# Token sums kept whole in DRAM and loaded ahead, two gate pairs held on chip, and a reset order in a decoder block on one core

## The chip, the core and the metric

The kernel runs on one core of one Trainium2 chip. The core has four compute engines that run their own instruction streams in order: TensorE (PE, matrix products; the page lists its weight loads apart as PEld), VectorE (DVE), ScalarE (ACT) and GpSimd (POOL). SyncE (SP) issues most of the transfers between DRAM and on-chip memory, POOL and ACT can issue some too. The metric is the device time of one execution in microseconds, lower is better, as the median of several runs. Time before: 1531.62 us (three runs, 1530.86 to 1532.0).

## What is computed

One decoder block over 1024 tokens with 16 learned meta tokens ahead (1040 positions of width 1024), all in float32:

```python
h = layer_norm(concat([meta, x]), ln0)
u_s5, q, k, v, o_pre, i_pre, f_pre, g_s5, g_m = split(h @ w_in + b_in)
z    = gelu(s5(u_s5)) @ s5_w_glu                  # grouped complex state-space scan
y_s5 = z[..., :D] * sigmoid(z[..., D:])
q, k = silu(causal_conv(q, k))                    # 4 taps
hm   = head_norm(mlstm(q, k, v, i_pre, f_pre))    # chunkwise, 4 heads
y_m  = (sigmoid(o_pre) * hm) @ m_w_out
mix  = sigmoid(g_s5) * y_s5 + sigmoid(g_m) * y_m
h    = layer_norm(ALPHA * h + mix @ w_o, ln1)
h    = layer_norm(ALPHA * h + square(relu(h @ w_up + b_up)) @ w_down, ln2)
return h without the meta positions
```

## The kernel before, in words

**Precision.** Each large product is made of float32 parts that PE takes: a number x is split into a high part (an ACT copy to the rounded type) and a low part (a DVE subtract, x minus its high part). A product is then three matmuls, high by high (L254), low by high (L255) and high by low (L256). Weights arrive raw (`wraw`), and ACT and DVE split them (`split_act`, L984 and L985: `gmwh` high, `gmwl` low; L234 and L235: `whi`, `wlo`). The activations after the first layer norm are kept on chip, transposed, as `hT_hi` and `hT_lo`, and also whole in DRAM as `h_dr`.

**Jobs.** The combined projection is cut into jobs that run one after the other in the order of the table `ORDER`: `q0` to `q3` (query and key), `v0` to `v3`, `u0` to `u3` (input of S5), `o0` to `o7` (some output gates), and the twelve pairs of gate tiles of which `a4` to `a11` and `b4` to `b11` treat eight. The GLU products (`glu`), the output products of the mLSTM (`ym`) and the two feed-forward matrices follow.

**Gate pairs by seven products.** A pair p of weight tiles against four quarters of the tokens is computed with seven products instead of eight, from sums of weight quarters (`wsums`) and sums of token quarters. Job `a{p}` loads the raw weights, forms the weight sums, writes two of them (`n1`, `r1`) to `gw_dr`, and runs products 1 to 3: 1 leaves an intermediate in `gme` (ACT), 2 gives a finished quarter that goes through a sigmoid into the buffer `gso` (one buffer) and from there to `sig_dr`, 3 adds to the intermediate (DVE), which goes to `e_dr`. Job `b{p}` loads `gw_dr` (two transfers of 512 KB) and `e_dr` back, splits the weights, and runs products 6, 5, 4 and 7, whose sums DVE adds into `gme` and `gmx`; ACT applies the sigmoid and SP writes to `sig_dr`. Product 4 of a job runs inside the next b-job.

**Token sums.** The generator `t_prep` makes the four token sums from `h_dr` early in the kernel (four chunks: load `tpr`, `quarter_sums` on DVE, split on ACT and DVE into `tpo`, write 512 KB to `t_dr`). Where the a-jobs end, `hT_hi` and `hT_lo` are overwritten block by block with these sums: `t_load(n)` loads the high and the low part of sum n from `t_dr`, 1 MB each, issued on POOL, straight into their place. Products 1, 2 and 3 of the last three a-jobs (`TAIL`) are therefore run block by block across the three jobs (all products 2, then all products 3), with a `t_load` behind each block.

**Work beside the jobs.** Other work is put between the matmuls by "lanes" of generators: the convolution (`cv`, first tap by ACT, three by DVE), the mLSTM (`ml`; `hraw` is its output, normalised in halves on ACT and DVE), S5 (`s5`, `s5c`; `s5Mx<-s5Kt` are 16 small transfers on SP, `s5Z`, `s5T`, `s5w` its scans on DVE), `t_prep` and `ah_scale` (`ah`), the gating of the mLSTM output (`hg`) and early work on the up matrix (`up`). `PACE`, the lists `ML` to `Y5` and `TPW` say how much matmul time passes between two steps of a lane, `LANE_AT` at which job a lane starts. On each engine the instructions then run in program order, but for a priority offset that a few places set; tiles come from a shared pool of slots of 30 buffers, and an instruction that takes a slot waits for its last user.

**Head.** The tables `LOAD0` (order of the first loads: x tiles, constants, weights) and `LN0_PROG` (the instructions of the first layer norm, written out by hand: s statistics, g aggregate, q root, c Newton step, n normalise, T transposes, a or v evacuation by ACT or DVE, X warm-up transposes of the identity, M matmuls of the first jobs) set the first 40 us.

Of the kernel before, what the change touches and what calls it, by code (L numbers as in the profile page):

```python
# [52 lines left out]
ML = [2.875, 1.882, 2.242, 5.227]  # L53
NL = [0.405, 2.68, 1.573, 2.414]
C5 = [1.273, 1.307, 2.211, 0.57]
K5 = [0.432, 8.726, 1.267, 8.96]
Z5 = [1.092, 0.624, 1.003, 0.401]
D5 = [3.696, 1.28, 0.806, 0.265]
W5 = [3.019, 1.105, 5.553, 0.851]
Y5 = [2.738, 1.285, 2.648, 4.789]  # L60
# [18 lines left out]
BLK = ((0, 256), (256, 640), (640, 1040))  # L79
BLK0 = (  # L80
# [49 lines left out]
def decoder_block(  # L130
# [24 lines left out]
    def f32(ap):  # L155
        return ap.bitcast(F32)
# [112 lines left out]
    t_dr = dram.tile([4, P, 2, 4, 512], F32, name="t_dr")  # L269
# [789 lines left out]
    def t_prep():  # L1059
        for c in range(4):  # L1060
            r = [slot("tpr"), slot("tpr")]
            for i in range(2):
                c0 = META + (c + 4 * i) * P
                nc.sync.dma_start(r[i][:, :D].rearrange("p (k s) -> p k s", k=KT), h_dr[:, :, c0:c0 + P])
            yield TPW
            quarter_sums(r[0], r[1])
            yield 3.0
            for n, x in ((2, r[1][:, 512:1024]), (3, r[1][:, 0:512]), (1, r[0][:, 0:512]), (4, r[0][:, 512:1024])):
                o = slot("tpo", F32R)
                a_.activation(o[:, 0:512], x, AF.Copy)  # L1070
                v_.tensor_tensor(o[:, 512:1024], x, f32(o[:, 0:512]), op=OP.subtract)
# [30 lines left out]
    def gate_out(p, i, half, x):  # L1102
        nc.sync.dma_start(sig_dr[2 * p + i, :, 512 * half:512 * half + 512], x)

    GA, GB = {}, {}

    def ga_prep(p):
        def prep(raw):
            r0, r1 = raw
            n1, n2 = wsums(r0[:, 0:512], r0[:, 512:1024], r1[:, 0:512], r1[:, 512:1024])  # L1110
            nc.sync.dma_start(gw_dr[p, 0], n1[:, :D])
            nc.sync.dma_start(gw_dr[p, 1], r1[:, :D])
            hi, lo = split_act(r0, "gmw")
            o = slot("gmo", F32R)
            a_.activation(o[:, 0:512], n2[:, 0:512], AF.Copy)
            v_.tensor_tensor(o[:, 512:1024], n2[:, 0:512], f32(o[:, 0:512]), op=OP.subtract)
            return {1: (hi[:, 0:512], lo[:, 0:512]), 2: (hi[:, 512:1024], lo[:, 512:1024]), 3: halves(o)}
        return prep

    def ga_step(p, n):  # L1120
        w, e, ps = GA[p]
        if n == 1:
            GA[p][2] = ps = mmps()
            gate_mm(ps, w[1], 0, 0, True)
            a_.activation(e[:, 0:512], ps, AF.Copy)
        elif n == 2:
            gate_mm(ps, w[2], 1, 0, False)
            x = mid.tile([P, 512], F32, tag="gso", bufs=1, name="gso")
            a_.activation(x, ps, AF.Sigmoid, bias=bft[:, gate_tile(p):gate_tile(p) + 1])
            gate_out(p, 0, 0, x)  # L1130
        else:
            px = mmps()
            gate_mm(px, w[3], 1, 1, True)
            v_.tensor_tensor(e[:, 512:1024], px, e[:, 0:512], op=OP.add)
            nc.sync.dma_start(e_dr[p], e[:, :D])

    def ga_job(p):
        def run(job):
            GA[p] = [job.w, slot("gme"), None]
            if p == TAIL[0]:  # L1140
                t_load(2)
            if not A_AFT:
                job.after()
# [99 lines left out]
    def ln0_load(t):  # L1243
        c0, n = rows0(t)
        xt = slot("x0")
        if t == 0:
            nc.sync.dma_start(xt[:META, :D], meta)
            nc.sync.dma_start(xt[META:, :D], x[0:P - META, :])
# [843 lines left out]
```

## Time and profile before

| | |
|---|---|
| median of three runs | 1531.62 us |
| the profiled execution | 1530.02 us |
| its span | 1528.3 us |
| mean granted clock of TensorE | 0.995 |
| busy: PE, DVE, ACT, POOL | 98%, 70%, 42%, 7% of the span |
| transferred | 324.92 MB, 213 GB/s mean |

The busy share tells how much of the span an engine was executing. An engine at 98% can be sped up only where it idles, so one looks for the stretches with idle time, then for what ended each wait. The granted clock is the share of full speed that the throttle allowed. A row of a timeline gives start, duration, engine, line, operation, output and inputs, and in brackets the idle time before it with the engine or transfer that ended it. The prediction quotes those rows.

### The profile page before, as it was taken

The numbers are of one execution on the slowest core, as the hardware profiler recorded it, in microseconds if no ns is written. First come the engines' busy times: TensorE is split into PE (matmuls) and PEld (weight loads), VectorE is DVE, ScalarE is ACT, GpSimd is POOL, SyncE is SP. The second block draws the span as 40 slices with busy tenths as digits, with TensorE's granted clock in tenths as the row PEclk, the third lists the DMA queues.
The fourth block names the chain that finished last, engine by engine and source line by source line (L and its number), as shares of the span: only waits on it lengthen the run. The fifth ranks groups of instructions, "written<-read, shape, count | busy, mean of one in ns | idle before, by whom it ended". The sixth has DMA issues, their size and how long they took to land.

```text
span 1528.3 us, 20822 instructions
## 1 busy us (share of the span) xinstructions
PE 1503.1 (98%) x7604; PEld 1270.7 (83%) x7604; DVE 1064.4 (70%) x1966; ACT 647.8 (42%) x1024; POOL 104.8 (7%) x178
## 2 busy tenths in 40 slices
PE   9999999999999799999999999999999999999997
PEld 9999989998888578888888888888888888888886
DVE  7487855786978665476677675766666689756786
ACT  6634552425345344332253253444444524433340
POOL 0000011523204100000000001000000000000000
PEclk9999999999999999999999999999999999999999
DMA  9417560405749998999692247544443897766642
GB/s 326 139 47 206 170 208 32 143 6 180 241 155 343 310 369 320 372 338 360 238 391 84 96 128 251 193 152 145 151 144 131 285 380 269 257 228 228 213 170 107
DMA packets 164343, 324.92 MB, mean 213 GB/s; under 512 B 19896, under 2 KB 70528, under 8 KB 164240
## 3 DMA queue, kind: packets, MB, share of 16 engines
q1 hardware_dynamic: 156992, 304.18, 58.0%
q0 software_dynamic: 7248, 19.40, 4.2%
q8 instruction: 60, 0.98, 0.3%
q14 instruction: 43, 0.35, 0.1%
HBM read 210.54 MB, written 111.81 MB: 211 GB/s over the span
## 4 chain that ended last, share of the span: by engine, by line
PE 89%; DMA 5%; DVE 2%; ACT 1%; SPq 1%; POOL 1%; issue 1%; DVEq 0%; POOLq 0%; ACTq 0%
PE mm L256 21%; PE mm L254 21%; PE mm L255 21%; PE sd L254 6%; PE sd L255 6%; PE sd L256 6%; PE mm L250 2%; DMA x<-in_x_dram 1%; PE pn L524 1%; PE pn L525 1%; PE pu L528 1%; DMA hm_dr<-hmF 1%; DMA tpr<-h_dr 1%; DMA s5yc<-ys_dr 1%; DMA ys_dr<-s5Y 1%
## 5 line engine op out<-in xcount | busy, mean ns | idle before, releaser
L254 PE MATMUL mm<-hT_hi,whi 128*128 128x512 f32 (+3 forms) x416 | 153.9, 370 | 0.0
L256 PE MATMUL mm<-hT_hi,wlo 128*128 128x512 f32 (+3 forms) x416 | 151.9, 366 | 0.0
L255 PE MATMUL mm<-hT_lo,whi 128*128 128x512 f32 (+3 forms) x416 | 151.5, 364 | 0.0
L255 PE MATMUL sd<-dwl,dah 128*128 128x512 f32 (+1 forms) x256 | 98.9, 386 | 0.0
L254 PE MATMUL sd<-dwh,dah 128*128 128x512 f32 (+1 forms) x256 | 98.9, 387 | 0.0
L256 PE MATMUL sd<-dwh,dal 128*128 128x512 f32 (+1 forms) x256 | 98.5, 385 | 0.0
L1785 ACT ACTIVATE dah<-da 128x1024 fp32r<-128x1024 f32 x56 | 58.6, 1051 | 90.2 <-PE sd L255 39.9
L1789 ACT ACTIVATE dwh<-wdr 128x1024 fp32r<-128x1024 f32 x56 | 58.9, 1053 | 79.3 <-DMA wdr<-in_wdn_dram 29.9
L255 PEld LDWEIGHTS mm<-hT_lo,whi 128*128 128x128 f32 x416 | 78.3, 188 | 10.6 <-issue 0.7
L254 PEld LDWEIGHTS mm<-hT_hi,whi 128*128 128x128 f32 x416 | 78.3, 188 | 9.9
L256 PEld LDWEIGHTS mm<-hT_hi,wlo 128*128 128x128 f32 x416 | 78.1, 188 | 10.0
L1786 DVE TENSOR_TENSOR dal<-da,dah 128x1024 fp32r<-128x1024 f32 x56 | 68.1, 1219 | 23.5 <-ACT dah L1785 23.5
L254 PE MATMUL mm<-hT_hi,gmwh 128*128 128x512 f32 x192 | 77.7, 407 | 5.0 <-ACT gmwh L984 2.5
L256 PE MATMUL mm<-hT_hi,gmwl 128*128 128x512 f32 x192 | 76.6, 404 | 5.3 <-DVE gmwl L985 5.3
L255 PE MATMUL mm<-dwl,dah 128*128 128x512 f32 (+1 forms) x208 | 80.0, 385 | 0.0
L254 PE MATMUL mm<-dwh,dah 128*128 128x512 f32 (+1 forms) x208 | 79.9, 385 | 0.0
L256 PE MATMUL mm<-dwh,dal 128*128 128x512 f32 (+1 forms) x208 | 79.7, 384 | 0.0
L255 PE MATMUL mm<-hT_lo,gmwh 128*128 128x512 f32 x192 | 76.6, 399 | 0.0
L1790 DVE TENSOR_TENSOR dwl<-wdr,dwh 128x1024 fp32r<-128x1024 f32 x56 | 68.2, 1219 | 10.2 <-ACT dwh L1789 9.6
L256 PE MATMUL mm<-whi,hT_lo 128*128 128x256 f32 (+1 forms) x256 | 74.4, 291 | 0.0
L254 PE MATMUL mm<-whi,hT_hi 128*128 128x256 f32 (+1 forms) x256 | 73.9, 289 | 0.0
L255 PE MATMUL mm<-wlo,hT_hi 128*128 128x256 f32 (+1 forms) x256 | 73.8, 288 | 0.0
(494 smaller groups left out, 3960.9 us busy)
## 6 DMA issues: line engine op xcount, KB each, us to landing
da<-act_dr SPq DMA_DIRECT2D x56, 512.0 KB, 5.2
wdr<-in_wdn_dram SPq DMA_DIRECT2D x56, 512.0 KB, 5.4
wraw<-in_wf_dram SPq DMA_DIRECT2D x36, 512.0 KB, 6.2
wur<-in_wup_dram SPq DMA_DIRECT2D x32, 512.0 KB, 4.4
act_dr<-upy SPq DMA_DIRECT2D x64, 256.0 KB, 2.7
wu_dr<-wpre SPq DMA_DIRECT2D x21, 512.0 KB, 5.4
wpre<-wu_dr POOLq DMA_DIRECT2D x21, 512.0 KB, 5.6
t_dr<-tpo SPq DMA_DIRECT2D x16, 512.0 KB, 5.2
```

The source lines that it names most:

```text
L250: t_.matmul(ps, tm[i], tm[j], start=(w == 0 and k == 0), stop=(w == 2 and k == n - 1))
L254: t_.matmul(ps, ah, bh, start=(i == 0 and part[0]), stop=False, skip_group_check=skip)
L255: t_.matmul(ps, ah, bl, start=False, stop=False, skip_group_check=skip)
L256: t_.matmul(ps, al, bh, start=False, stop=(i == n - 1 and part[1]), skip_group_check=skip)
L524: t_.matmul(pn[:, :257], qi[:, c0:c0 + n], Cs[c][:, :257], start=True, stop=False)
L525: t_.matmul(pn[:, :257], sws[c], vt[c][:, :257], start=False, stop=True)
L528: t_.matmul(pu[:, :257], kws[c][:n], vt[c][:n, :257], start=True, stop=True)
L1785: a_.activation(ah[:, :D], a[:, :D], AF.Copy)
L1786: v_.tensor_tensor(alo[:, :D], a[:, :D], f32(ah[:, :D]), op=OP.subtract)
L1789: a_.activation(wh, raw[i], AF.Copy)
L1790: v_.tensor_tensor(wl, raw[i], f32(wh), op=OP.subtract)
```

## The change

- The token sums are written to `t_dr` whole (256 KB instead of 512 KB a write); the split moves from `t_prep` to `t_load`. `t_fetch` loads a sum on SP into two slots `ttr`, one block ahead, and `t_load` splits them (two ACT copies and two DVE subtracts of 128x1024 per sum, with a priority offset) into the block of `hT_hi` and `hT_lo` that was just used.
- `HELD`: the pairs of the first two b-jobs, where they belong to `TAIL`, keep `n1`, `r1` and `gme` in their slots; nothing of them is written to or read from `gw_dr` and `e_dr`.
- `ORDER`: o1 before o0; the a-jobs end with a7 a8 a11 a10 a9 (were a8 a7 a9 a10 a11); the b-jobs run b10 b11 b9 b5 b8 b6 b4 b7 (were b4 b9 b5 b10 b8 b6 b7 b11). `t_prep` starts at q3 instead of v1, and several paces and start points are other numbers.
- The first convolution tap and all `hraw` normalisations go to DVE.
- Head: x0 comes in two column halves, with the meta rows issued on ACT; the other loads are in another order; the warm-up transposes are 41 + 18 + 1 instead of 57 + 20; some evacuations move from ACT to DVE.

```diff
-ORDER = '... o0 o1 ... u3 a8 a7 a9 a10 a11 b4 b9 b5 b10 b8 b6 b7 b11'
-HMO_AT = 2
+ORDER = '... o1 o0 ... u3 a7 a8 a11 a10 a9 b10 b11 b9 b5 b8 b6 b4 b7'
+HMO_AT = 1
+HOLD = 2
+TF = 1
+TFA = 1
+TLA = 0
+T_UP = 200
-UPD = 1
-TPW = 4.0
+UPD = 0
+TPW = 6.0
-LANE_AT = {'t_prep': 'v1', 'hm_gate': 'b5', 'ah_scale': 'glu2', 'up_early': 'ym3'}
-PACE = {'ml': 0.56, 'cv': 0.315, 's5': 1.0, 's5c': 0.729, 's5g': 2.2, 'ah': 1.549, 'up': 0.623, 'hg': 2.974}
+LANE_AT = {'t_prep': 'q3', 'hm_gate': 'b9', 'ah_scale': 'glu2', 'up_early': 'ym2'}
+PACE = {'ml': 0.56, 'cv': 0.08, 's5': 1.0, 's5c': 0.656, 's5g': 2.2, 'ah': 1.961, 'up': 0.685, 'hg': 2.974}
...
-CV0 = 1
-HRA = 1
+CV0 = 0
+HRA = 0
-LOAD0 = "x0 c0 w0 x1 w1 c1 x2 w2 x3 w3 x4 x5 x6"
+LOAD0 = "x0 c0 x1 w1 x2 w0 c1 w2 x3 w3 x6 x5 x4"
...
@@ t_prep
-                o = slot("tpo", F32R)
-                a_.activation(o[:, 0:512], x, AF.Copy)
-                v_.tensor_tensor(o[:, 512:1024], x, f32(o[:, 0:512]), op=OP.subtract)
-                nc.sync.dma_start(t_dr[n - 1, :, :, :, c * P:(c + 1) * P],
-                                  f32(o[:, 0:1024]).rearrange("p (h k s) -> p h k s", h=2, k=4))
-                yield 1.2
+                nc.sync.dma_start(t_dr[n - 1, :, :, c * P:(c + 1) * P], x.rearrange("p (k s) -> p k s", k=4))
+            yield 1.2
...
+    TR = {}
+
+    def t_fetch(n):
+        TR[n] = [slot("ttr"), slot("ttr")]
+        for j, r in enumerate(TR[n]):
+            nc.sync.dma_start(r[:, :D].rearrange("p (k s) -> p k s", k=2), t_dr[n - 1, :, 2 * j:2 * j + 2, :])
+
     def t_load(n):
         kh, half = TB[n]
         c = slice(META + 512 * half, META + 512 * half + 512)
-        for z, x in enumerate((hT_hi, hT_lo)):
-            g_.dma_start(x[:, 4 * kh:4 * kh + 4, c], t_dr[n - 1, :, z])
+        with tc.high_priority(offset=T_UP):
+            for j, r in enumerate(TR.pop(n)):
+                d = slice(4 * kh + 2 * j, 4 * kh + 2 * j + 2)
+                r3 = r[:, :D].rearrange("p (k s) -> p k s", k=2)
+                a_.activation(hT_hi[:, d, c], r3, AF.Copy)
+                v_.tensor_tensor(hT_lo[:, d, c], r3, f32(hT_hi[:, d, c]), op=OP.subtract)
+        later = [2, 1, 3, 4][[2, 1, 3, 4].index(n) + TF:]
+        if later:
+            t_fetch(later[0])
...
@@ ga_prep
-            nc.sync.dma_start(gw_dr[p, 0], n1[:, :D])
-            nc.sync.dma_start(gw_dr[p, 1], r1[:, :D])
+            if p in HELD:
+                HELD[p] = [n1, r1]
+            else:
+                nc.sync.dma_start(gw_dr[p, 0], n1[:, :D])
+                nc.sync.dma_start(gw_dr[p, 1], r1[:, :D])
...
@@ ga_job
-            if p == TAIL[0]:
+            if p == T_AT[0]:
+                for n in [2, 1, 3, 4][:TF]:
+                    t_fetch(n)
+            if p == T_AT[1]:
                 t_load(2)
...
@@ ln0_load
-            nc.sync.dma_start(xt[:META, :D], meta)
-            nc.sync.dma_start(xt[META:, :D], x[0:P - META, :])
+            for c0, c1 in HALF:
+                a_.dma_start(xt[:META, c0:c1], meta[:, c0:c1])
+                nc.sync.dma_start(xt[META:, c0:c1], x[0:P - META, c0:c1])
...
+    A_ALL = [int(w[1:]) for w in ORDER.split() if w[0] == "a"]
+    TAIL = A_ALL[-3:]
+    T_AT = A_ALL[-3 - TFA], A_ALL[-3 - TLA]
+    HELD.update({p: None for p in [int(w[1:]) for w in ORDER.split() if w[0] == "b"][:HOLD] if p in TAIL})
```

The order in which the instructions now stand shows in three places. The first is PE's order in the head, from the second row of the program on; `warm` are the warm-up transposes, `ln` the transposes of x tiles 0 (`x_109`), 1 (`x_115`) and so on. Before:

```order
L1331 MATMUL warm<-ident 128x128 x57
L1305 MATMUL ln_219<-ident,x_109 128x128 x4
L1305 MATMUL ln_220<-ident,x_109 128x128 x4
L1331 MATMUL warm<-ident 128x128 x20
L1305 MATMUL ln_270<-ident,x_115 128x128 x4
L1305 MATMUL ln_271<-ident,x_115 128x128 x4
```

Now, at the same place:

```order
L1360 MATMUL warm<-ident 128x128 x41
L1334 MATMUL ln_205<-ident,x_109 128x128 x4
L1334 MATMUL ln_206<-ident,x_109 128x128 x4
L1360 MATMUL warm<-ident 128x128 x18
L1334 MATMUL ln_250<-ident,x_115 128x128 x4
L1360 MATMUL warm<-ident 128x128
L1334 MATMUL ln_251<-ident,x_115 128x128 x4
```

The two large warm-up blocks are shorter, and one warm-up transpose stands between the halves of tile 1.

The second is SP's queue where the a-jobs end: `sig_dr<-gso` is the write of a finished gate quarter, `s5Mx<-s5Kt` the small S5 transfers. Before:

```order
L831 DMA s5Mx<-s5Kt 16x4x64 x2
L831 DMA s5Mx<-s5Kt 16x4x48 x2
L831 DMA s5Mx<-s5Kt 16x4x32 x2
L831 DMA s5Mx<-s5Kt 16x4x16 x2
L1103 DMA sig_dr<-gso 128x512
L216 DMA wraw<-gw_dr 128x1024 x2
L1165 DMA gme<-e_dr 128x1024
```

Now, up to the first of the s5Mx transfers and a little beyond:

```order
L1118 DMA sig_dr<-gso 128x512
L1156 DMA e_dr<-gme 128x1024
L221 DMA wraw<-in_wf_dram 128x1024 x2
L1091 DMA ttr<-t_dr 128x1024 x2
L1118 DMA sig_dr<-gso 128x512
L836 DMA s5Mx<-s5Kt 16x4x128 x2
L836 DMA s5Mx<-s5Kt 16x4x112
L1129 DMA gw_dr<-wus 128x1024
L1130 DMA gw_dr<-wraw 128x1024
```

The write of that gate quarter stands ahead of the s5Mx transfers, the loads of the weights and intermediate of the first b-job are gone, and loads of token sums (`ttr`) stand ahead of it.

The third is DVE's order in the first b-jobs: `gme` and `gmx` are sums of products, `gmwl` low parts of weights, `s5w` and `s5Z` S5's sums and scans. Before, in the job b4 (`gme_5590`):

```order
L1184 TENSOR_TENSOR gme_5590<-mm_5828,gme_5590 128x512
L888 TENSOR_TENSOR s5Z_5679<-s5w_5741,s5w_5742 128x520
L889 TENSOR_TENSOR s5Z_5679<-s5w_5741,s5w_5742 128x520
L894 SCALAR_TENSOR_TENSOR s5w_5741<-s5_r8_2992,s5Z_5679 128x130 x4
L1187 TENSOR_TENSOR gme_5590<-mm_5847,gme_5590 128x512
L894 SCALAR_TENSOR_TENSOR s5w_5741<-s5_r8_2992,s5Z_5679 128x130 x4
L904 TENSOR_TENSOR s5Z_5679<-s5w_5741,s5T_5617 128x512
L907 TENSOR_TENSOR s5w_5742<-s5w_5741,s5T_5617 128x512
L985 TENSOR_TENSOR gmwl_5821<-wraw_5585,gmwh_5820 128x1024
```

Now, in the job b10 (`gme_5480`), with the last subtract of token sum 4 (`hT_lo`) ahead:

```order
L888 TENSOR_TENSOR s5w_5687<-s5Z_5619,s5T_5551 128x520
L891 TENSOR_TENSOR s5w_5688<-s5Z_5619,s5T_5551 128x520
L1101 TENSOR_TENSOR hT_lo_89<-ttr_5664,hT_hi_88 128x2x512
L889 TENSOR_TENSOR s5w_5688<-s5Z_5619,s5T_5551 128x520
L890 TENSOR_TENSOR s5w_5687<-s5Z_5619,s5T_5551 128x520
L1212 TENSOR_TENSOR gme_5480<-mm_5772,gme_5480 128x512
L893 TENSOR_TENSOR s5Z_5619<-s5w_5687,s5w_5688 128x520
L894 TENSOR_TENSOR s5Z_5619<-s5w_5687,s5w_5688 128x520
L1215 TENSOR_TENSOR gme_5480<-mm_5791,gme_5480 128x512
L899 SCALAR_TENSOR_TENSOR s5w_5687<-s5_r8_2930,s5Z_5619 128x130 x5
L990 TENSOR_TENSOR gmwl_5765<-wus_5316,gmwh_5764 128x1024
L899 SCALAR_TENSOR_TENSOR s5w_5687<-s5_r8_2930,s5Z_5619 128x130 x3
```

The S5 block still stands among the sums of the first b-job; a token-sum subtract is new ahead of them, and the low weight part that follows is that of the second b-job, taken from a held tile (`wus_5316`).

More of the change, by code (lines that the diff above doesn't have):

```diff
@@ L40 @@
 MAGIC = 1.5 * 2 ** 23
-ORDER = 'q0 q1 v0 v1 q3 q2 o0 o1 o3 v2 o2 u0 u1 v3 o5 u2 o4 o7 a5 a6 a4 o6 u3 a8 a7 a9 a10 a11 b4 b9 b5 b10 b8 b6 b7 b11'
-HMO_AT = 2
+ORDER = 'q0 q1 v0 v1 q3 q2 o1 o0 o3 v2 o2 u0 u1 v3 o5 u2 o4 o7 a5 a6 a4 o6 u3 a7 a8 a11 a10 a9 b10 b11 b9 b5 b8 b6 b4 b7'
+HMO_AT = 1
 HS = 2
+HOLD = 2
[3 more added lines that the diff above has]
+T_UP = 200
 HGD = 2
-UPD = 1
-TPW = 4.0
+UPD = 0
+TPW = 6.0
 S5_START = 'o2'
-LANE_AT = {'t_prep': 'v1', 'hm_gate': 'b5', 'ah_scale': 'glu2', 'up_early': 'ym3'}
-PACE = {'ml': 0.56, 'cv': 0.315, 's5': 1.0, 's5c': 0.729, 's5g': 2.2, 'ah': 1.549, 'up': 0.623, 'hg': 2.974}
+LANE_AT = {'t_prep': 'q3', 'hm_gate': 'b9', 'ah_scale': 'glu2', 'up_early': 'ym2'}
+PACE = {'ml': 0.56, 'cv': 0.08, 's5': 1.0, 's5c': 0.656, 's5g': 2.2, 'ah': 1.961, 'up': 0.685, 'hg': 2.974}
 SPLIT_UP = 50
@@ L52 @@
 ZD = 1
[L53 to L60, printed above, removed]
-CV0 = 1
-HRA = 1
+ML = [2.875, 1.694, 2.242, 5.227]
+NL = [0.324, 2.948, 1.416, 2.414]
+C5 = [1.146, 1.176, 1.99, 0.23]
+K5 = [0.475, 9.599, 1.742, 10.842]
+Z5 = [1.081, 0.618, 0.993, 0.496]
+D5 = [3.696, 1.28, 0.645, 0.254]
+W5 = [3.019, 1.105, 4.998, 0.681]
+Y5 = [2.738, 0.771, 2.648, 4.789]
+CV0 = 0
+HRA = 0
 A_AFT = 0
@@ L268, in decoder_block @@
     h_dr = dram.tile([P, KT, LEN], F32, name="h_dr")
-    t_dr = dram.tile([4, P, 2, 4, 512], F32, name="t_dr")
+    t_dr = dram.tile([4, P, 4, 512], F32, name="t_dr")
     e_dr = dram.tile([12, P, 1024], F32, name="e_dr")
@@ L1103, in gate_out @@
         nc.sync.dma_start(sig_dr[2 * p + i, :, 512 * half:512 * half + 512], x)
-    GA, GB = {}, {}
+    GA, GB, HELD = {}, {}, {}
     def ga_prep(p):
@@ L1134, in ga_step @@
             v_.tensor_tensor(e[:, 512:1024], px, e[:, 0:512], op=OP.add)
-            nc.sync.dma_start(e_dr[p], e[:, :D])
+            if p in HELD:
+                HELD[p].append(e)
+            else:
+                nc.sync.dma_start(e_dr[p], e[:, :D])
     def ga_job(p):
@@ L1162, in gb_prep @@
     def gb_prep(p, raw):
-        n1, r1 = raw
-        e = slot("gme")
-        nc.sync.dma_start(e[:, :D], e_dr[p])
+        if p in HELD:
+            n1, r1 = HELD[p][:2]
+            e = None
+        else:
+            n1, r1 = raw
+            e = slot("gme")
+            nc.sync.dma_start(e[:, :D], e_dr[p])
         (h1, l1), (h2, l2) = split_act(n1, "gmw"), split_act(r1, "gmw")
@@ L1204, in run @@
             last = list(GB)
-            GB[p] = dict(w=job.w, e=job.w.pop("e"))
+            GB[p] = dict(w=job.w, e=job.w.pop("e") or HELD[p][2])
             if not B_AFT:
@@ L1216, in run @@
                 gb_flush()
-        all_jobs.append(Job([(gw_dr[p, i], 1024) for i in range(2)], run))
+        all_jobs.append(Job([] if p in HELD else [(gw_dr[p, i], 1024) for i in range(2)], run))
         all_jobs[-1].prep = lambda raw: gb_prep(p, raw)
@@ L1420, in up_early @@
                 yield 3.0
-    TAIL = [int(w[1:]) for w in ORDER.split() if w[0] == "a"][-3:]
+    A_ALL = [int(w[1:]) for w in ORDER.split() if w[0] == "a"]
+    TAIL = A_ALL[-3:]
+    T_AT = A_ALL[-3 - TFA], A_ALL[-3 - TLA]
+    HELD.update({p: None for p in [int(w[1:]) for w in ORDER.split() if w[0] == "b"][:HOLD] if p in TAIL})
     B_END = [int(w[1:]) for w in ORDER.split() if w[0] == "b"][-1]
```

20 rows, old and new, of the table LN0_PROG are left out of this document.

## The prediction

> **What bounds the kernel now.** The page's first two parts, read first, show TensorE (PE) as the bound.
>
> ```profile
> PE 1503.1 (98%) x7604; PEld 1270.7 (83%) x7604; DVE 1064.4 (70%) x1966; ACT 647.8 (42%) x1024; POOL 104.8 (7%) x178
> PE   9999999999999799999999999999999999999997
> ```
>
> Only one inner slice is a 7, so I asked for busy time by stretch around it (PE, PEld, DVE, ACT, POOL, then granted clock, DMA share, GB/s).
>
> ```profile
> 458.40:496.60 38.20, 36.93 (x188) 30.69 (x188) 31.12 (x64) 22.59 (x34) 17.00 (x18) 1.00 1.01 343
> 496.60:534.80 38.20, 28.53 (x125) 21.73 (x123) 23.08 (x48) 14.09 (x23) 5.19 (x10) 0.90 1.02 310
> 534.80:573.00 38.20, 37.42 (x171) 30.51 (x170) 23.05 (x29) 18.89 (x22) 0.00 (x0) 0.96 1.02 369
> 573.00:611.20 38.20, 38.20 (x166) 30.86 (x165) 20.90 (x25) 17.09 (x19) 0.00 (x0) 1.00 0.89 321
> 611.20:1490.00 878.80, 878.80 (x3824) 712.31 (x3824) 608.82 (x864) 348.89 (x533) 11.14 (x21) 1.00 0.64 226
> ```
>
> From 573 to 1490 us PE is never idle, so nothing can be gained there. The first three rows hold the step from the a-jobs to the b-jobs: PE idles 1.27 + 9.67 + 0.78 = 11.7 us. The clock of 0.90 and 0.96 instead of 1.00 stands for about 2 x (3.8 + 1.5) = 10.7 us at half clock. PE's waits name the releasers.
>
> ```profile
> PE mm L256 <- DVE gmwl L985: 5.3, 1, 5.3
> PE mm L254 <- ACT gmwh L984: 2.5, 1, 2.5
> PE mm L254 <- ACT gso L1129: 1.1, 1, 1.1
> PE pS L514 <- DVE sw L516: 1.0, 1, 1.0
> PE mm L254 <- DVE gmx L1191: 0.8, 1, 0.8
> PE mm L254 <- ACT gme L1125: 0.7, 1, 0.7
> ```
>
> The timelines of PE, ACT, DVE and SP there show why (start, duration, idle before and releaser).
>
> ```profile
> 526.48 0.50 PE L254 MATMUL mm<-hT_hi,gmwh 128*128 128x512 f32 x1 [2.48 <-ACT gmwh L984]
> 527.28 0.61 PE L255 MATMUL mm<-hT_lo,gmwh 128*128 128x512 f32 x1
> 533.24 0.79 PE L256 MATMUL mm<-hT_hi,gmwl 128*128 128x512 f32 x1 [5.35 <-DVE gmwl L985]
> 533.83 0.63 PE L254 MATMUL mm<-hT_hi,gmwh 128*128 128x512 f32 x1
> 534.26 0.63 PE L255 MATMUL mm<-hT_lo,gmwh 128*128 128x512 f32 x1
> ```
>
> ```profile
> 512.24 0.69 ACT L1129 ACTIVATE gso<-mm,bft 128x512 f32<-128x512 f32 x1 [8.71 <-DMA sig_dr<-gso]
> 524.79 0.69 ACT L1129 ACTIVATE gso<-mm,bft 128x512 f32<-128x512 f32 x1 [1.93 <-DMA sig_dr<-gso]
> 525.38 1.04 ACT L984 ACTIVATE gmwh<-wraw 128x1024 fp32r<-128x1024 f32 x1
> 529.49 1.37 DVE L894 TENSOR_TENSOR_SCAN s5w<-s_r,s5Z 128x130 f32<-128x130 f32 x4
> 531.97 1.21 DVE L985 TENSOR_TENSOR gmwl<-wraw,gmwh 128x1024 fp32r<-128x1024 f32 x1
> 498.03 6.97 SPq L831 DMA_DIRECT2D s5Mx<-s5Kt  x11
> 505.10 0.71 SPq L1103 DMA_DIRECT2D sig_dr<-gso  x1
> ```
>
> The single gso buffer's write to DRAM stood behind 16 s5Mx transfers on SP, so ACT stood 8.71 us and everything behind it came late. The next gso stood too (1.93 us), its gmwh followed at 525.38, and that weight's low part came at 531.97, behind the S5 scans in DVE's order. Matmuls came 0.43 us apart at half clock (533.83 to 534.26) against 38.20 / 166 = 0.23: 527.3 + 10.7 is 538, so from 533.2 on ten or eleven were slow and lost 2.0 us. The step loses 11.7 + 2.0 = 13.7 us.
>
> **The change, part by part.**
>
> *Held pairs.* b10 and b11 now come first, and their four weight tiles and two intermediates stay on chip; the splits of b10 stand far ahead of their use. Eight transfers of weights and four of intermediates, 6.3 MB, go; the token loads lose another 4.2 MB. Their bytes alone are worth nothing (PE is full beside a DMA share of 0.89). What goes is the wait for late weights, 2.48 + 5.35, and with the sig_dr write now ahead of the s5Mx transfers, the block of 8.71 on ACT.
>
> *New waits in the step.* Eight ACT copies and eight DVE subtracts (by the gmwh and gmwl rows 1.04 and 1.21 us each, 8.3 and 9.7 in all) now stand in these engines' order ahead of gso, gme and gmwl, and each waits for its ttr load. I followed the new order from 477 us on with before's durations. What is late next: (1) s5k behind s5Mi on ACT, 1.9 us; (2) gso of a8 and gme of a11 behind the splits of token sum 2, 1.1 us (the nearest rows, 1.1 + 0.7, give 1.8 as a bound, 0 the other); (3) the seventh product of b10 behind gme on DVE, which stands behind the last subtract and the S5 sums, 3.0 us (0 if the loads land early, 5.35 as before if late); (4) gmwl of b11 behind S5 scans, 1.1 us. I let the stalls of under 1 us behind (3) vanish in it. Sum 7.1.
>
> *Half clock.* The clock fell at 527.28 (0.61 us for a matmul), behind the wait of 2.48 and ahead of that of 5.35, so by this trace a wait of 2.5 us is enough, and (3) is longer. I charge one stretch a third of the 10.7 us long, full of work: 3.5 / 0.43 = 8 matmuls x 0.20 = 1.6 us; bounds 0, and all 10.7, 25 x 0.20 = 5.0. The Trainium skill, "TensorE: Matmul & The Clock Gate", section "HAM oscillation — how this bites in real kernels", warns only of idle gaps above about 3.4 us. By that rule the 1.6 would fall away and the forecast below would be 1522.7; in this trace the fall came after 2.48, so I keep the row.
>
> The step then loses 7.1 + 1.6 = 8.7 instead of 13.7: **a gain of 5.0**, from -6 (rival three) to 13.7.
>
> *Token sums.*
>
> ```profile
> L1070 ACT ACTIVATE tpo<-tpr x16: 614/618/627, 114.6 to 202.6; 128x512 fp32r<-128x512 f32 x16
> L1071 DVE TENSOR_TENSOR tpo<-tpr,tpo x16: 657/682/693, 117.8 to 204.3; 128x512 fp32r<-128x512 f32 x16
> hT_hi<-t_dr POOLq DMA_DIRECT2D x4, 1024.0 KB, 15.3
> wraw<-gw_dr SPq DMA_DIRECT2D x16, 512.0 KB, 7.6
> ```
>
> 16 x 0.62 on ACT and 16 x 0.68 on DVE (9.9 and 10.9 us) leave the stretch 115 to 205 us, where PE is nearly full. They pay only through PE's wait for sw (1.0): DVE had quarter sums ahead of it. The preparation now starts at q3 and is paced wider, so I take that 1.0 as gone (0 to 1.0). The eight POOL transfers hid and are worth 0; if the SP loads that take their place land as late as 15.3 instead of 7.6, that is rival three.
>
> *Moved to DVE.* Eight convolution taps, sixteen hraw normalisations:
>
> ```profile
> L562 DVE TENSOR_SCALAR hraw<-hraw,hmv,hny x16: 405/407/412, 166.9 to 491.7; 128x256 f32<-128x256 f32 x16
> ```
>
> 16 x 0.41 = 6.5 us, and for the taps at the same length 3.3, over some 400 us, beside PE; 0, and 1 if a product waits for each longest of them.
>
> *Head.*
>
> ```profile
> 0.74 0.39 SPq L1247 DMA_DIRECT2D x<-in_meta_dram  x1
> 1.19 0.41 SPq L1248 DMA_DIRECT2D x<-in_x_dram  x1
> 5.19 1.29 DVE L1265 BATCH_NORM_STATS2 ln_s<-x 128x6 f32<-128x512 f32 x2 [3.48 <-DMA x<-in_x_dram]
> 9.46 1.29 DVE L1265 BATCH_NORM_STATS2 ln_s<-x 128x6 f32<-128x512 f32 x2 [0.60 <-DMA x<-in_x_dram]
> 9.52 1.04 PE L1305 MATMUL ln<-ident,x 128*128 128x128 f32 x8
> 10.40 2.35 PE L1331 MATMUL warm<-ident 128*128 128x128 f32 x20
> 13.39 1.07 PE L1305 MATMUL ln<-ident,x 128*128 128x128 f32 x8 [0.65 <-PE warm L1331]
> ```
>
> Meta moves to ACT's queue, so x0's bytes start 1.19 - 0.74 = 0.45 earlier; in halves, one statistic (1.29 / 2 = 0.65) runs while the second half lands. That is 1.1 us at the first transposes (9.52). x1 goes out ahead of w0 and two warm-up blocks shrink by 17 x 2.35 / 20 = 2.0 us, so the second transposes (13.39) can follow: **1.3 us**, between 0.45 and 2.0. The Trainium skill, "DMA: Bandwidth & Descriptors", section "Issuing engines are not separate DMA queues", says that a second issuing engine saves only the issue time. By it the head gains 0.45 and the forecast would be 1525.2; no row here has a tile in halves, and the statistic's overlap does not rest on bandwidth, so I stay at 1.3.
>
> *Other order and paces.* Before 458 us PE has small waits only; I give them 0, plus or minus 2.
>
> Sum: 5.0 + 1.0 + 1.3 = 7.3 us. The profiled execution took 1530.02 us (span 1528.3 and 1.7 around it), so 1522.7; the median of the runs, 1531.62, lies 1.6 above it: **1524.3 us**.
>
> **Rivals.**
> 1. *Waits gone entirely.* The loads land early, DVE works through the splits in its idle time (23.08 of 38.20 us busy), no wait over 1 us is left: 13.7 + 1.0 + 1.3 = 16.0, 1515.6 us. For it: held weights need no load. Against: sixteen split steps in the same stretch.
> 2. *Wait for wait.* The splits delay b10's gme sums by as much as the late weights did; the step loses 13.7 again and only head and sw come: 1529.3 us. For it: the same S5 block still stands in DVE's order.
> 3. *Slower: token sum 4 late.* Its ttr loads go out only after slots are freed by PE, in SP's order, where DMA is saturated (1.01, 1.02). ACT and DVE wait in order for it, with gso, gme and gmwl behind. If it lands after 15.3 instead of 7.6 us, PE stands 7.7 longer, and the whole stretch at half clock is worked through, 5.0 instead of 1.6: 11.1 on top of the forecast, 1535.4. The kernel is slower than before once the load is over 3.9 us later than I take it (7.3 - 3.4), by over 0.2% from 7.0 us on. Against: those 15.3 are of 1 MB from POOL, with other rows at 7.6.
>
> **How the numbers follow.** Forecast 0.50, rival one 0.14, two 0.18, three 0.18. 0.2% of the time, 3.1 us, is about what a measurement of this kernel can tell from no change. Forecast and rival one lie beyond it, with 0.04 of rival two: faster 0.68; the rest of rival two is same, 0.14; slower 0.18. The forecast's own range is 1519 to 1528 (half clock 0 or 5.0, head 0.45 to 2.0, small waits 2). The range reaches to rival one's 1515.6 and, for the milder part of rival three, to 1534.
>
> **What would show it.** Right: no gmwh wait at the first b-job, no gso block of 8 us on ACT, PE idle of some 7 us between 458 and 573, the first transposes near 8.4 us. Wrong: a PE wait above 5 us behind hT_lo, gme or gso; a granted clock under 0.9 in the step; or idle PE after 573, which none of my terms has.

## The result and the profile after

The changed kernel takes 1521.63 us (median of four runs, 1521.46 to 1524.2) against 1531.73 us before: a ratio of 0.9939, 95% interval 0.9922 to 0.9956, 10.1 us faster. A second series of five (in the last experiments) gave 1520.09 against 1530.33, 0.9936 (0.9924 to 0.9947). The profiled execution took 1521.50 us, its span 1519.7. Several variants below scatter by 3 to 8 us from run to run, so differences of 1 us between two of them are not read as differences.

The page's first two parts after the change: busy time of each engine, and PE's busy tenths in 40 slices.

```profile
PE 1499.7 (99%) x7587; PEld 1268.7 (83%) x7587; DVE 1083.3 (71%) x1994; ACT 625.8 (41%) x978; POOL 96.0 (6%) x170
PE   9999999999999999999999999999999999999997
```

The 7 in the slice at 500 us has become a 9. Busy time by stretch (PE, PEld, DVE, ACT, POOL, granted clock, DMA share, GB/s):

```profile
38.20:458.40 420.20, 417.41 (x2666) 382.95 (x2665) 306.79 (x802) 169.96 (x283) 64.57 (x119) 1.00 0.43 130
458.40:496.60 38.20, 35.84 (x170) 29.06 (x169) 31.57 (x57) 21.36 (x32) 15.94 (x16) 0.96 0.87 280
496.60:534.80 38.20, 34.76 (x158) 28.35 (x158) 33.93 (x65) 22.09 (x30) 2.42 (x4) 0.96 0.59 195
534.80:573.00 38.20, 38.20 (x180) 31.46 (x179) 27.09 (x35) 21.96 (x25) 0.00 (x0) 1.00 0.96 348
```

In the step from the a- to the b-jobs (rows two to four) PE idles 2.36 + 3.44 + 0 = 5.8 us, 11.7 before. The clock of 0.96 in two rows stands for 2 x (1.5 + 1.5) = 6.1 us at half clock, some 14 matmuls x 0.2 = 2.9 us. The step loses 8.7 us, 13.7 before. Where DMA ran at a share of 1.02 in the row at 500 us it now runs at 0.59; DVE's load there rose from 23.08 to 33.93 of 38.20 us. PE's longest waits are one of 3.4 us for gme on DVE and one of 2.4 us for gme on ACT. The waits for gmwl (5.3) and gmwh (2.5) are gone, and so are those for sw (1.0; one of 0.3 is left elsewhere) and gmx (0.8). Between 38 and 458 us, though, PE idles 420.20 - 417.41 = 2.79 us, and 2.87 before: other small waits have come there. PE's timeline at these two waits:

```profile
486.92 0.40 PE L260 MATMUL mm<-hT_lo,gmwh 128*128 128x512 f32 x1
489.68 0.79 PE L259 MATMUL mm<-hT_hi,gmwh 128*128 128x512 f32 x1 [2.36 <-ACT gme L1143]
490.27 0.63 PE L260 MATMUL mm<-hT_lo,gmwh 128*128 128x512 f32 x1
525.21 0.50 PE L259 MATMUL mm<-hT_hi,gmwh 128*128 128x512 f32 x1 [3.44 <-DVE gme L1212]
526.70 0.61 PE L259 MATMUL mm<-hT_hi,gmwh 128*128 128x512 f32 x1
```

Behind the first wait the matmuls take 0.6 instead of 0.4 us for about 3 us: half clock. Behind the second they run at 0.4 until 526.7 and then at 0.6 until 530.1. The timeline of DVE ahead of the second wait, and of ACT ahead of the first, shows what stood in the queue:

```profile
520.77 0.70 DVE L888 TENSOR_TENSOR s5w<-s5Z,s5T 128x520 f32<-128x520 f32 x1
521.38 0.69 DVE L891 TENSOR_TENSOR s5w<-s5Z,s5T 128x520 f32<-128x520 f32 x1
521.99 1.22 DVE L1101 TENSOR_TENSOR hT_lo<-ttr,hT_hi 128x1024 fp32r<-128x1024 f32 x1
523.13 0.69 DVE L889 TENSOR_TENSOR s5w<-s5Z,s5T 128x520 f32<-128x520 f32 x1
523.74 0.69 DVE L890 TENSOR_TENSOR s5w<-s5Z,s5T 128x520 f32<-128x520 f32 x1
524.46 0.69 DVE L1212 TENSOR_TENSOR gme<-mm,gme 128x512 f32<-128x512 f32 x1
488.51 0.63 ACT L1133 ACTIVATE gmo<-wus 128x512 fp32r<-128x512 f32 x1 [1.98 <-DVE wus L1420]
489.05 0.58 ACT L1143 ACTIVATE gme<-mm 128x512 f32<-128x512 f32 x1
```

PE has run out of work at 521.77 (525.21 - 3.44) and waits for the first sum of b10, which is made at 524.46, because DVE takes four S5 products and the last token-sum subtract first. The first wait is ACT's: gme of a11 stands behind gmo, and gmo waits 1.98 us for the weight sums, which DVE makes behind the subtracts of token sum 2.

In the head the first statistics start at 4.14 (5.19 before), and the transposes follow:

```profile
4.14 1.29 DVE L1294 BATCH_NORM_STATS2 ln_s<-x 128x6 f32<-128x512 f32 x2 [2.43 <-DMA x<-in_x_dram]
7.49 1.04 PE L1334 MATMUL ln<-ident,x 128*128 128x128 f32 x8
11.37 0.63 PE L1334 MATMUL ln<-ident,x 128*128 128x128 f32 x4 [0.87 <-PE warm L1360]
```

### The profile page after: what moved, and what is told of

Read it like the earlier page. It is cut to its first block, busy times and chain, and to the rows that moved or that the text cites. A ratio compares the mean times of both kernels' runs of the same rounds, so it can differ in the third digit from the quotient of the medians.

```text
span 1519.7 us, 20723 instructions
## 1 busy us (share of the span) xinstructions
PE 1499.7 (99%) x7587; PEld 1268.7 (83%) x7587; DVE 1083.3 (71%) x1994; ACT 625.8 (41%) x978; POOL 96.0 (6%) x170
## 4 chain that ended last, share of the span: by engine, by line
PE 65%; DVE 1%; DMA 1%; ACT 0%; POOL 0%; issue 0%; DVEq 0%; SPq 0%; ACTq 0%
PE mm L259 16%; PE mm L261 16%; PE mm L260 16%; PE sd L259 6%; PE sd L260 6%; PE sd L261 6%; DMA ttr<-t_dr 1%; PE ln L1609 0%; DVE gmwl L990 0%; DVE hT_lo L1101 0%; ACT gelf L945 0%; PE s5y L929 0%; DVE arow L1919 0%; PE s5y L928 0%; ACT L945 0%
```

## The experiments

All ratios are to the kernel before, run beside each variant on the same chip; the changed kernel stands at 0.9939 and 0.9936.

**1. The head alone**, in the kernel before:

```diff
-LOAD0 = "x0 c0 w0 x1 w1 c1 x2 w2 x3 w3 x4 x5 x6"
+LOAD0 = "x0 c0 x1 w1 x2 w0 c1 w2 x3 w3 x6 x5 x4"
...
+            for c0, c1 in HALF:
+                a_.dma_start(xt[:META, c0:c1], meta[:, c0:c1])
+                nc.sync.dma_start(xt[META:, c0:c1], x[0:P - META, c0:c1])
```

(and the new `LN0_PROG`). 

> The kernel before with the new head alone (x0 in column halves, meta on ACT, the new load order, 41 + 18 + 1 warm-up transposes). My theory: PE is the bound from the first products on and what the head gains early (first transposes 7.49 instead of 9.52, first large product 30.5 instead of 31.65, 2.4 us by 114 us in the traces) is carried to the end: 2.0 to 2.5 us below before, about 1529.4. Rival: the step at 500 us is paced by saturated transfers, so the head's gain is swallowed there by longer waits: 1531.7, within 0.5 us of before.

Measured: 1528.54 us, ratio 0.9987 (0.9978 to 0.9995), 2.0 us faster by the ratio. The head's gain reaches the end, though the step's waits move about: the wait for gmwl grew from 5.3 to 6.6 us.

**2. The token sums the old way**, in the changed kernel:

```diff
-                nc.sync.dma_start(t_dr[n - 1, :, :, c * P:(c + 1) * P], x.rearrange("p (k s) -> p k s", k=4))
-            yield 1.2
+                o = slot("tpo", F32R)
+                a_.activation(o[:, 0:512], x, AF.Copy)
+                v_.tensor_tensor(o[:, 512:1024], x, f32(o[:, 0:512]), op=OP.subtract)
+                nc.sync.dma_start(t_dr[n - 1, :, :, :, c * P:(c + 1) * P], ...)
+                yield 1.2
...
+        for z, x in enumerate((hT_hi, hT_lo)):
+            g_.dma_start(x[:, 4 * kh:4 * kh + 4, c], t_dr[n - 1, :, z])
```

> The changed kernel with the token sums the old way (split in t_prep, high and low parts in DRAM, 1 MB loads on POOL straight into place), everything else as changed. My theory: the 3.4 us wait of b10 behind DVE and its half clock (1.4) come from the eight splits, so they shrink, and about 1 us comes back for the splits at 115 to 205 us; the loads hide: 1518 to 1522, so whole sums are worth little or less than nothing by themselves. Rival: loading ahead is what made the step short; the 1 MB loads (15.3 us from issue to landing before) make PE wait 3 to 8 us: 1525 to 1530.

Measured: 1532.13 us, ratio 1.0008 (0.9998 to 1.0018): the whole gain is gone. PE's waits:

```profile
PE mm L259 <- DMA hT_hi<-t_dr: 4.6, 1, 4.6
PE s5k L818 <- POOL s5Rr L805: 2.8, 1, 2.8
PE pt L574 <- DVE hraw L567: 2.7, 1, 2.7
```

The rival was right on the loads (4.6 us in the step; `hT_hi<-t_dr` is the load of a high part). But the two other waits lie at 283 and 299 us: with four pace steps a chunk and the new pace of 1.961, the preparation runs on to 309 us, into the S5 preparation. So this run mixes two causes, and the fifth separates them.

**3. Nothing held:**

```diff
-HOLD = 2
+HOLD = 0
-ORDER = '... b10 b11 b9 b5 b8 b6 b4 b7'
+ORDER = '... b5 b8 b10 b11 b9 b6 b4 b7'
```

> The changed kernel with nothing held (all eight pairs through DRAM) and b5 b8 as first b-jobs (b10 cannot be first when its weights go through DRAM): b5 b8 b10 b11 b9 b6 b4 b7. My theory: the first b-job's weights come late again and PE waits for gmwh and gmwl at its start as before (2.5 + 5.4, with half clock 2): 5 to 9 us slower than the changed kernel, 1527 to 1531. Rival: the sig_dr write ahead of the s5Mx transfers and the paces made the gain, and holding is worth nothing: 1521 to 1523.

Measured: 1525.44 us, ratio 0.9969 (0.9958 to 0.9980), about 4.5 us of the gain gone (0.9969 against 0.9939 and 0.9936). The wait for late weights is back, in part:

```profile
PE mm L261 <- DVE gmwl L990: 3.2, 1, 3.2
```

Holding, with the job order that it allows, is worth some 4 to 5 us here, a little under the lower end of what I expected. The order moved with it in this run, so the two are not separated.

**4. The write of gso out of SP's queue**, in the kernel before:

```diff
-            gate_out(p, 0, 0, x)
+            gate_out(p, 0, 0, x, a_)
```

> The kernel before, with the write of the gate quarter in gso issued on ACT instead of SP, so that it no longer stands behind the 16 s5Mx transfers. My theory: ACT's block of 8.71 us goes and with it PE's waits for gso, gme and gmwh (1.1 + 0.7 + 2.5); the wait of 5.35 for gmwl stays in part because it stands behind the S5 scans in DVE's order: 3 to 5 us faster than before, 1527 to 1529. Rival one: the block was the whole cause, all 13.7 us go: 1518 to 1520. Rival two: the loads of b4's weights, which stand behind the same transfers, are the cause, and nothing changes: 1531 to 1532.

Measured: 1536.88 us, ratio 1.0041 (1.0027 to 1.0054): slower by 6 us, which none of the three had. ACT's block of 8.71 us is gone (the gso of 512.24 now runs at 505.30). PE's waits, ACT ahead of the second of them, and the load of token sum 1's high part (KB, us from issue to landing), last of all the same load in the kernel before:

```profile
524.96 0.79 PE L254 MATMUL mm<-hT_hi,gmwh 128*128 128x512 f32 x1 [5.41 <-DMA hT_hi<-t_dr]
534.22 0.79 PE L254 MATMUL mm<-hT_hi,gmwh 128*128 128x512 f32 x1 [4.47 <-ACT gmwh L984]
547.95 0.50 PE L254 MATMUL mm<-hT_hi,gmwh 128*128 128x512 f32 x1 [2.57 <-DMA hT_hi<-t_dr]
532.74 0.33 ACTq L1103 DMA_DIRECT2D sig_dr<-gso  x1
533.11 1.06 ACT L984 ACTIVATE gmwh<-wraw 128x1024 fp32r<-128x1024 f32 x1 [13.04 <-DMA s5yc<-ys_dr]
hT_hi<-t_dr POOLq DMA_DIRECT2D x1, 1024.0 KB, 18.6
```

```profile
hT_hi<-t_dr POOLq DMA_DIRECT2D x1, 1024.0 KB, 9.8
```

Two things came with the edit. First, the loads themselves took longer. Token sum 1's high part landed at 524.9 (issued at 506.26) instead of 513.8 (issued at 503.98), while PE was ready for it at 519.55 (524.96 - 5.41), only 1.4 us earlier than in the kernel before (520.96). POOL's queue, which loads the sums, moved 2.02 of 2.54 MB in the kernel before from 504 to 512 us, and 1.12 of 2.98 MB here from 508 to 516. The likely reason, argued and not tested alone, is that while ACT stood, the transfers that depend on its work were not issued yet and left the DMA to this load. Second, the write now stands in ACT's own order. The third one was issued only at 532.74, and gmwh behind it started after 13.04 us of idle time, put down to an s5yc transfer of S5; that is PE's wait of 4.47. So the run moves the block to another place, and does not show what its removal alone would be worth.

**5. As the second, with one pace step a chunk:** `yield 1.2` behind the loop. 

> As the second experiment (token sums the old way in the changed kernel), but with one pace step per chunk of t_prep as in the changed kernel instead of four, so that its sixteen splits no longer drag on to 309 us into the S5 preparation. My theory, from the trace of the second experiment: of its 10 us, 8 were lost at 280 to 300 us by that overlap and 2 to 3 in the step by PE's wait of 4.6 us for the 1 MB load of token sum 4; here the first part goes and the second stays: 1523 to 1526. Rival: the split work itself (10 us on ACT and on DVE) is what costs, wherever it stands: 1529 to 1533.

Measured: 1523.19 us, ratio 0.9954 (0.9942 to 0.9967). My theory's number holds, by other parts. The load waited for here, as in the second run, is that of token sum 3 (issued at 512.89, landed 12.8 us later), and not of token sum 4 as I had taken it. Two rows of the step by stretch, and PE's two waits:

```profile
458.40:496.60 38.20, 36.90 (x193) 31.05 (x193) 32.99 (x64) 21.15 (x32) 16.52 (x18) 1.00 0.83 281
496.60:534.80 38.20, 36.23 (x174) 29.70 (x173) 30.36 (x61) 17.16 (x25) 5.95 (x10) 1.00 1.03 269
PE pu L533 <- ACT kw L516: 2.8, 1, 2.8
PE mm L259 <- DMA hT_hi<-t_dr: 2.0, 1, 2.0
```

In the step this execution idles 1.30 + 1.97 = 3.3 us at full clock: it loses 5.4 less there than the changed kernel (8.7). So the splits do cost what the prediction feared, DVE and ACT queues in the step. But at 217 us four split copies in a row, 2.19 us in all, stand on ACT ahead of kw (weighted keys of the mLSTM), and PE waits 2.8. The old way pays there: PE idles 5.5 us between 38 and 458 us, 2.8 in the changed kernel. The 2 us by which this run lies above the changed kernel are at the edge of what the two intervals tell apart.

**6. The new token sums alone**, in the kernel before (t_prep, t_fetch and t_load of the changed kernel). 

> The kernel before with the token sums alone changed (whole in DRAM, fetched a block ahead, split in place); old order, nothing held, old paces and head. My theory: the loads are taken out of PE's way and SP's order around them changes, but the first b-job's weights still come through DRAM behind DVE's S5 work, so about half of the step's 13.7 us goes: 1524 to 1528. Rival one: the loads hid in before anyway, and the new splits only add to ACT and DVE: 1530 to 1534. Rival two: the sums are the whole gain in the step: 1520 to 1523.

Measured: 1528.39 us, ratio 0.9988 (0.9979 to 0.9997), 1.8 us faster by the ratio: less than half of what I expected of it. The waits that are left in its step are gme (2.9, on ACT) and gmwl (2.8), the second that of weights that come from DRAM.

**7. S5's last products later:**

```diff
+        if b == 3:
+            yield 6.0
         c, s = T[:, 0:520], T[:, 520:1040]
```

> The changed kernel with 6 us more pace ahead of S5's last block of DVE products (s5w), so that these stand behind the last token-sum subtract and nearly behind the first gme sum of b10 in DVE's order. My theory: the wait of 3.4 us behind gme in b10 and the 1.4 us of half clock behind it go: 4 to 5 us faster than the changed kernel, 1517 to 1518. Rival: the wait comes from the landing of token sum 4 and only changes its releaser, or the S5 block delays the next b-jobs' weights instead: within 1.5 us of the changed kernel, 1520.5 to 1523.

Measured: 1521.30 us, ratio 0.9942 (0.9930 to 0.9955): no gain, the rival. The wait behind gme is gone and stands one product further on:

```profile
524.63 0.69 DVE L1214 TENSOR_TENSOR gme<-mm,gme 128x512 f32<-128x512 f32 x1
529.47 2.66 DVE L901 TENSOR_TENSOR_SCAN s5w<-s_r,s5Z 128x130 f32<-128x130 f32 x8
535.78 0.50 PE L259 MATMUL mm<-hT_hi,gmwh 128*128 128x512 f32 x1 [3.10 <-DVE gmx L1221]
```

All eight scans now stand together ahead of gmx.

**8. a11's first product ahead of a10's splits:**

```diff
-            if not A_AFT:
+            if not A_AFT and p != TAIL[0]:
                 job.after()
             ga_step(p, 1)
-            if A_AFT:
+            if A_AFT or p == TAIL[0]:
                 job.after()
```

> The changed kernel with the weight splits of a10 put behind the first product of a11, so that a11's gme copy stands ahead of gmwh and gmo in ACT's order. My theory: PE's wait of 2.4 us for that copy at 487 us and the half clock behind it (1.3 us) go, minus up to 1 us if a10's weights come later: 2.5 to 3.7 us faster than the changed kernel, 1518 to 1519. Rival: a10's low part then comes too late and PE waits for gmwl instead: no gain, 1521 to 1524.

Measured: 1523.12 us, ratio 0.9950 (0.9936 to 0.9964): the rival. The wait for gme fell from 2.4 to 0.8, and the one of b10 from 3.4 to 0.7 without being aimed at; waits for gmwh (2.8 in two) and gmwl (2.0) took their place.

**9. The old token sums, their splits spread** (`yield 0.3` behind each). 

> The changed kernel with the token sums the old way (split in t_prep, 1 MB loads on POOL), and the sixteen splits spread with a pace of 0.3 each, so that they neither bunch on ACT (the fifth experiment: four in a row at 217 us, PE waited 2.8 us for kw behind them) nor drag on to 309 us (the second). My theory: the step from a- to b-jobs is bound by what stands on DVE and ACT there, and the eight splits of the changed kernel are the excess; with them gone the step loses 4 to 5 us instead of 10, and the wait at 217 us goes too: 1518 to 1520. Rival: the splits find another product to hold up between 160 and 260 us, and loads of 1 MB make PE wait in the step: 1522 to 1526.

Measured: 1525.14 us, ratio 0.9970 (0.9959 to 0.9980), runs from 1522.1 to 1530.1: the rival. The wait for kw is gone, hraw (1.5) and sw (1.4) wait instead, and the step loses more than in the fifth:

```profile
525.84 0.76 PE L259 MATMUL mm<-hT_hi,gmwh 128*128 128x512 f32 x1 [4.71 <-DVE s5Z L911]
hT_hi<-t_dr POOLq DMA_DIRECT2D x1, 1024.0 KB, 15.6
```

This product does not read s5Z. The second row is the load of token sum 3's high part: issued at 510.12, it landed 15.6 us later, at 525.7, just ahead of this product, and that is what PE waited for. Between the second, fifth and ninth run, which differ in the pace of work over 200 us earlier, this load took 15.9, 12.8 and 15.6 us, and the wait at this place was 4.6, 2.0 and 4.7.

**10. Less DVE work in the step**: two of the four s5w products, both sums and all scans of S5's last block are left out. 

> The changed kernel without part of the DVE work of S5's last block (two of its four s5w products, both sums and all eight scans are left out: 5.5 us of DVE, 2.1 of it ahead of the first gme sum of b10); nothing else is changed. My theory: DVE's sum of work in the step is the bound, so the wait behind gme shrinks by 2 us or vanishes with its half clock: 2 to 5 us faster than the changed kernel, 1517 to 1519.5. Rival: the wait is set by the landing of token sum 4 in DVE's order, ahead of which nothing is gained: 1521 to 1522.

Measured: 1519.84 us, ratio 0.9937 (0.9925 to 0.9949), the same as the changed kernel beside it. My theory, that DVE's sum of work in the step is the bound, falls: DVE is busy 88.8 us in the three rows of the step instead of 92.2 (eleventh run), and the time is the same. The timeline of DVE and PE:

```profile
521.41 0.68 DVE L912 TENSOR_TENSOR s5Z<-s5w,s5T 128x512 f32<-128x512 f32 x1
522.02 0.69 DVE L915 TENSOR_TENSOR s5w<-s5w,s5T 128x512 f32<-128x512 f32 x1
522.73 0.69 DVE L1215 TENSOR_TENSOR gme<-mm,gme 128x512 f32<-128x512 f32 x1
523.48 0.79 PE L259 MATMUL mm<-hT_hi,gmwh 128*128 128x512 f32 x1 [3.49 <-DVE gme L1215]
```

The place ahead of gme was filled with S5's next products. Nor does DVE wait for token sum 4, the rival: its last subtract starts at 519.67 with no idle time ahead. What decides here is which instructions stand ahead of gme in the order, not how much DVE has to do.

**11. The changed kernel again.** 

> The changed kernel itself beside these and the kernel before, for the comparison of the small differences: 1521 to 1523, 8 to 10 us below before.

Measured: 1520.09 us, ratio 0.9936 (0.9924 to 0.9947), as expected.

**12. The paces of before** in the changed kernel (`PACE`, `TPW`, `LANE_AT`, `ML` to `Y5`, `CV0`, `HRA`, `UPD`, `HMO_AT`). 

> The changed kernel with the paces and lane starts of before (PACE, TPW, LANE_AT but for hm_gate at the third b-job, ML to Y5, UPD, HMO_AT, the first convolution tap and half of the hraw normalisations on ACT again); held pairs, whole sums, job order and head as changed. My theory: what stands on DVE ahead of a gme or gmwl in the step decides, and the paces set that; with before's numbers S5's blocks meet the token-sum splits elsewhere and the step loses 3 to 6 us more than with the new ones, and the wait for sw at 132 us (1.0) comes back: 1524 to 1528. Rival: held pairs, whole sums and head carry the whole gain and the paces are worth nothing: 1519.5 to 1522.

Measured: 1527.61 us, ratio 0.9983 (0.9974 to 0.9992), 7.0 us slower than the changed kernel by the ratios. The longest waits:

```profile
PE mm L259 <- DVE gme L1212: 4.1, 1, 4.1
PE mm L259 <- ACT gme L1143: 2.6, 1, 2.6
PE pk L514 <- ACT kw L516: 2.5, 1, 2.5
```

The mechanism I named explains about half. The two step waits are 0.7 and 0.2 us longer, PE idles 7.0 us in the step instead of 5.8, and one more stretch of 3.4 us runs at half clock (0.96 and 0.91 in the first two rows of the step), 8 matmuls x 0.20 = 1.6 us: 2.8 us in all. Between 38 and 458 us PE idles 5.3 us instead of 2.8. The wait for sw did not come back; the largest new one is for kw at 130 us. ACT holds kw behind s_sn, a sine of the S5 preparation, which waits 6.70 us for its argument s_th from DVE. DVE makes s_th at 131.65, behind the four subtracts of the token sums' quarters, after a wait of 1.90 us for their load (timeline of DVE and ACT):

```profile
128.46 0.69 DVE L1079 TENSOR_TENSOR tpr<-tpr 128x512 f32<-128x512 f32 x1 [1.90 <-DMA tpr<-h_dr]
...
131.65 0.17 DVE L675 TENSOR_SCALAR s_th<-s_th 128x16 f32<-128x16 f32 x1
131.85 0.22 ACT L677 ACTIVATE s_sn<-s_th 128x16 f32<-128x16 f32 x1 [6.70 <-DVE s_th L675]
```

About half of the price of the old paces lies far from the step.

## Why the prediction was right, and where it was not

The forecast was 1524.3 us, 7.3 below before; 10.1 (median) and 8.5 (profiled execution) were measured. Of the 2.7 us by which the median came out lower than forecast, 1.5 are the distance from the profiled execution to the median, 1.6 before and 0.1 now, which the forecast had taken over unchanged; this part is chance. By its own terms (5.0 the step, 1.0 sw, 1.3 the head) the sum measured 5.0 + 0.1 + 2.0 = 7.1 of the 8.5; the other 1.4 are not placed. The range of 1519 to 1528 does not follow from the bounds given with it: added up, these reach from 1520.0 to 1530.6.

- **The step's sum**, 8.7 us left of 13.7: it measured 8.7 in the profiled execution. Its parts came out otherwise. Wait (3), gme of b10 behind the last subtract and the S5 products, was forecast at 3.0 and measured 3.44 with the rows that were named. Waits (1) and (4) did not come; wait (2) was 2.36 in place of 1.1, and for another reason in part (gmo ahead of gme). So idle time was 5.8 instead of 7.1, and half clock 2.9 instead of 1.6, since both waits were followed by a stretch of 3.4 us of it and one had been charged. That the two sums are both 8.7 is luck: the errors cancel.
- **Half clock.** The row was kept against the rule of the Trainium skill ("TensorE: Matmul & The Clock Gate", section "HAM oscillation — how this bites in real kernels"), by which only gaps above about 3.4 us matter. The trace bore the row out: half clock followed a wait of 2.36. The rule's 1522.7 lies nearer to the measured time, but not because half clock stayed away.
- **Held pairs**: the cause as named. The third run bears it out (gmwl's wait is back, 4 to 5 us), with the job order changed beside it.
- **Token sums.** "The eight POOL transfers hid and are worth 0" was true of the trace of before: token sum 1's high part landed at 513.8, 7.2 us ahead of its first product, token sum 4's at 540.9, 2.1 us ahead. It was wrong as a price: where order and timing were others, runs four (5.41 + 2.57), two (4.6) and five (2.0) show PE waiting for them. The splits cost the step more than the loads in the fifth run and less in the second; alone, in the sixth, the new sums gain 1.8. The 1.0 for sw did not come: that wait is gone, but PE's idle time between 38 and 458 us is 2.79 us, 2.87 before.
- **Head**: forecast 1.3, measured 2.0 by the first run (0.8 to 3.4 by its interval); the transposes came at 7.49 and not at 8.4, and the first large product at 30.50 instead of 31.65. The mis-sized term is the first one: in the kernel before, tile 0's rows were normalised by 8.86, but the 57 warm-up transposes ran until about 9.5, so cutting 16 of them gave more than the earlier load alone. The Trainium skill's rule that a second issuing queue saves only the issue time ("DMA: Bandwidth & Descriptors", section "Issuing engines are not separate DMA queues") would have given 0.45. x0's first statistics did start 1.05 earlier, but with its halves, their order and the queue changed together; the rule itself was not tested.
- **Order and paces**, taken at 0, plus or minus 2: mis-sized. Put back alone, the old paces cost 7 us. The job order alone, and the new paces in the kernel before, were not run. The paces were fitted to where each lane's instructions fall among the others, so old paces with new splits are no neutral ground. The gains of single parts (2.0 the head, 1.8 the sums) and the losses when one is taken out (4.5 the held pairs, 7 the paces, 2 to 10 the sums) do not add up to 10.1, and need not: each decides what the next waits for.
- **Rival three** did not come: the ttr loads landed after 6.1 to 8.3 us, not 15. PE waited for none of them directly. That PE is not idle after 573 us held.

None of the variants beats the changed kernel. Two that aimed at its remaining 5.8 us of waits (seven and eight) moved them. What would free both at once stays open.

## What to carry to other kernels

A wait also holds back what is issued behind it. Before one is removed, list which transfers and products will then come earlier or meet others, and price those (run four: a load of 9.8 us took 18.6, and the write that was moved held up the engine it was moved to). On in-order engines beside a saturated one, ask which instructions stand ahead of the one that is waited for: taking work off the engine (run ten) let other work move into that place, and shifting a block (run seven) moved the wait one product on. Pace tables belong to the instruction order they were set with, and are measured together with it.

## What the runs showed of the hardware

Half clock does not follow from a wait's length alone. Two executions at the same place, a wait of 2.0 us in each: experiment eleven and then experiment ten, PE's timeline.

```profile
488.97 0.63 PE L259 MATMUL mm<-hT_hi,gmwh 128*128 128x512 f32 x1 [2.01 <-ACT gme L1143]
```

```profile
489.17 0.50 PE L259 MATMUL mm<-hT_hi,gmwh 128*128 128x512 f32 x1 [2.00 <-ACT gme L1146]
```

The first runs on at 0.63 us a matmul until 492.4, the second goes to 0.39 at once. The Trainium skill ("TensorE: Matmul & The Clock Gate", section "Part 1: The HAM clock gate (the "warmup" mystery)") has a window of activity that runs freely, of about 3.4 us; that would let the phase of the wait decide. The traces agree: in all fourteen, the half-clock stretches between the head and 1490 us last 3.41, 6.83 or 10.24 us, and they begin and end on a grid of 3.41 us that runs through the whole execution. Busy time by stretch of this grid (PE, PEld, DVE, ACT, POOL, granted clock, DMA share, GB/s), experiment eleven and then experiment ten:

```profile
485.78:489.18 3.40, 1.39 (x5) 0.53 (x5) 3.40 (x8) 1.60 (x4) 0.00 (x0) 1.00 0.98 306
489.20:492.59 3.39, 3.39 (x9) 2.61 (x9) 3.23 (x7) 1.41 (x2) 0.00 (x0) 0.50 0.69 253
```

```profile
485.38:488.78 3.40, 1.79 (x7) 0.85 (x5) 3.37 (x7) 1.79 (x4) 0.00 (x0) 1.00 1.02 317
488.80:492.19 3.39, 3.02 (x13) 2.49 (x14) 3.39 (x9) 1.85 (x3) 0.00 (x0) 1.00 0.62 232
```

In experiment eleven the wait lies wholly inside one stretch, PE idles 2.0 us of it, and the next stretch has half clock. In experiment ten a line of the grid falls into the wait, so 1.6 us lie ahead of it and 0.4 behind, and the clock stays. Over the fourteen traces, each of the 23 full-clock stretches with 1.8 us idle or more was followed by half clock, none of those with 1.5 us or less, and two of the nine between (one with 1.54, one with 1.71).
